# Weight casts, sums and the second spread at the end of the first attention take other places in the order

## The chip, the cores and the metric

The kernel runs on one core of one Trainium2 chip. The metric is the device time of one execution in microseconds (us), the median of several runs. The core has five engines that run side by side and meet at semaphores: TensorE (PE in the profile) multiplies, VectorE (DVE) and ScalarE (ACT) work on elements, GpSimd (POOL) and SyncE (SP) mostly issue transfers here. Each engine works off its own row of instructions strictly in the order in which they stand.

## What is computed

A model of two layers on 512 tokens of width 1024, in float32: a differential attention with a feed-forward block, then a sliding-window attention with sinks and a second feed-forward block. The change touches the end of the first attention. Cut to that:

```python
def one_block(args):                       # 128 queries of 8 heads, two maps c each
    s = jnp.einsum('bqhcd,bkhcd->bhcqk', qblk, k) * scale
    p = jax.nn.softmax(jnp.where(causal, s, NEG_INF), axis=-1)
    a = p[:, :, 0] - lam * p[:, :, 1]
    return jnp.einsum('bhqk,bkhe->bqhe', a, v)
...
o = rms_norm(o, subln) * (1.0 - lambda_init)
x = x + o.reshape(B, S, DA_V) @ w_o
x = x + swiglu(rms_norm(x, ffn_norm[l]), w_gate_up[l], w_down[l])
```

## The kernel before, in words

Every float32 product is made of three fast ones: each operand is split into a high part (`hi`, a cast on ScalarE) and a low part (`lo`, the rest, a subtraction on VectorE), and `mm3` (L295) multiplies high by high, high by low and low by high. Tokens are four blocks `t` of 128.

The first attention runs over four pairs of heads. For each pair a table of slots (`DA_STEPS`, for the last pair `DA_STEPS3`) gives the order of its steps on TensorE: T turns keys, C scores a block of queries, U transposes the differences of the two maps, W weighs the values, N sums the squares for the norm's root, B spreads the root over the rows. Between the steps other products are pulled in as filling. For the last pair the filling is the output projection of the first half (pairs 0 and 1, `o_da(0, ...)`, all four blocks) and of the second half (pairs 2 and 3, `o_da(1, ...)`) for blocks 0 and 1 once the outputs are there. Blocks 2 and 3 of the second half come behind the last step, mixed with the norms (`ffn.norm`) and turns (`ffn.turn`) of the feed-forward block, which then starts with `ffn.start`.

TensorE's row is as the code is written. VectorE's and ScalarE's rows are made by a scheduler: it goes by priorities (`tc.high_priority`) and by `tc.issue_after`, which puts an instruction behind another.

The names that the prediction speaks of, with lines:

- The **root**: `rsq` (L235 to L250), a chain of small VectorE steps on the sums `so` that ends in `ro`. `spread` (L1144) lets TensorE spread `ro` over the rows (`po`, L1148), and VectorE scales the output with it (`osb`, L1149).
- The **exponentials**: `soften` (L1077) gets the row maxima `mx` (taken by VectorE at L1071, scaled at L1080), ScalarE makes four exponentials of 128x512 for the last block of queries (L1084), VectorE the **difference** of the two maps (L1092). TensorE transposes it (L1108, banks `tr`), ScalarE and VectorE copy the result out as high and low parts (`aT`, L302 and L303). The next transposes into a bank wait for its copies. `weigh` (L1115) multiplies the values with `aT`.
- The **sums into x**: `o_block` (L457) multiplies one block into two banks `acc` (the halves `n` of the width), each with four pieces `j` of three products, and VectorE adds each bank to `xs` (L468).
- The **weight units**: `o_units` (L452) loads a half's part of `w_o` as four units of 128x2x512: pieces 0 and 1 for `n` = 0, the same for `n` = 1, pieces 2 and 3 for `n` = 0, then for `n` = 1. `load_w` (L281) issues each transfer into a raw buffer (L287), and `parts` makes two high parts (L269) and two low parts (L270) of it. The raw buffers form a ring of two, `tag="raw", bufs=RAWB` with `RAWB = 2` (L43): a transfer waits until the parts of the unit two before it are made.
- The **turned halves**: `transpose_in` (L310) turns a normed token block with TensorE (L314) and copies it out as `hTh` and `hTl` (L302, L303); `norm` (L520) squares on ScalarE (L526), takes a root, and multiplies on VectorE (L532). `start` (L594) is the first reader of the halves.

Of the kernel before, what the change touches and what calls it, by code (L numbers as in the profile page):

```python
# [40 lines left out]
HOT = 1220  # L41
# [71 lines left out]


# [23 lines left out]
def tile_yoco_hybrid(  # L138
# [96 lines left out]
    def rsq(dst, v, n):  # L235
        y = small([P, 32], "rsq_y", bufs=1)[:, 0:n] if n > 4 else small([P, 4], "rsq_s", bufs=2)[:, 0:n]
        w = small([P, 32], "rsq_w", bufs=1)[:, 0:n] if n > 4 else small([P, 4], "rsq_t", bufs=2)[:, 0:n]
        eng = nc.vector
        if n == 1:
            h = small([P, 1], "rsq_h")  # L240
            eng.tensor_scalar(h, v, -0.5, None, op0=ALU.mult)
        eng.tensor_scalar(w.bitcast(I32), v.bitcast(I32), 1, None, op0=ALU.logical_shift_right)
        eng.tensor_scalar(y.bitcast(I32), w.bitcast(I32), -1.0, float(0x5F3759DF), op0=ALU.mult, op1=ALU.add)
        for it in range(3):
            if n == 1:
                eng.tensor_scalar(w, y, y, h, op0=ALU.mult, op1=ALU.mult)
# [3 lines left out]
            eng.scalar_tensor_tensor(dst if it == 2 else y, w, 1.5, y, op0=ALU.add, op1=ALU.mult)  # L250

    class Split:

# [200 lines left out]
        return {(j, n): load_w([wv[:, k0 + j:k0 + j + 2, n * 512:(n + 1) * 512]], 2, 512)  # L454
                for j in (0, 2) for n in range(2)}

    def o_block(units, pieces, t, ready=None):  # L457
        while ready and not ready():
            yield None
        for n in range(2):  # L460
# [3 lines left out]
                mm3(pt, sh, sl, *units[j - j % 2, n].row(j % 2), j == 0, j == 3)  # L464
                yield 0.65
            xsl = xs[:, t, n * 512:(n + 1) * 512]
            with tc.high_priority(offset=HOT):
                nc.vector.tensor_tensor(xsl, xsl, pt, op=ALU.add)  # L468


    class Flow:
# [521 lines left out]
    class Pair:  # L993
# [83 lines left out]
        def soften(self, i):  # L1077
# [3 lines left out]
            for h in range(2):  # L1081
                for c in range(2):
                    g = 2 * h + c
                    nc.scalar.activation(sb[h][:, c, 0:n], sb[h][:, c, 0:n], AF.Exp, bias=mx[:, g:g + 1],  # L1084
                                         scale=self.scl[:, i, g:g + 1], accum_out=sm[:, g:g + 1])
            rs = small([P, 2], "rs2")
            nc.vector.reciprocal(rs, sm[:, 1::2])
            cl = small([P, 2], "cl")
            nc.vector.scalar_tensor_tensor(cl, rs, nlam, sm[:, 0::2], op0=ALU.mult, op1=ALU.mult)
            for h in range(2):  # L1090
                p0, p1 = sb[h][:, 0, 0:n], sb[h][:, 1, 0:n]
                nc.vector.scalar_tensor_tensor(p0, p1, cl[:, h:h + 1], p0, op0=ALU.mult, op1=ALU.add)  # L1092
            hf = i // 2
            if i % 2 == 0:
                self.eps[hf] = small([P, 4], "eps", bufs=3)
# [37 lines left out]
        def norm(self, hf):  # L1133
# [5 lines left out]
                nc.vector.scalar_tensor_tensor(so, pss[:, 0:8:2], 1.0 / P, self.eps[hf], op0=ALU.mult, op1=ALU.add)  # L1139
            self.ro = small([P, 4], "ro")  # L1140
            with tc.high_priority(offset=NPRI):
                rsq(self.ro, so, 4)

        def spread(self, hf):  # L1144
            pb = att("po")
# [15 lines left out]
    with tc.tile_pool(name="da", bufs=1, reuse_waits="tile") as ap:  # L1161
# [405 lines left out]
```

## Time and profile before

| what | before |
|---|---|
| median of 3 runs | 1122.76 us (1122.44 to 1123.15) |
| the profiled execution's own time | 1122.68 us |
| its span | 1120.6 us |
| busy in 225 to 275 us: PE, DVE, ACT | 47.52, 41.62, 26.17 us of 50 |
| last pair's last scores on TensorE | 229.85 us |
| first product of the second half's projection | 244.40 us |
| first product of the feed-forward block | 270.02 us |

In the order of time a row gives start, duration, engine, line, operation, output and inputs with their size, how many, and in brackets how long the engine had been idle before it and what ended the wait. In the table by stretches the columns are the stretch, its length, the busy time of PE, of its weight loads (PEld), DVE, ACT and POOL with the number of instructions, the granted clock of TensorE (1 is full), the busy share of the DMA engines and GB/s. L is a line of the kernel before.

### The profile page before, as it was taken

How to read it: one execution, taken by the hardware profiler on the slowest of the kernel's cores; microseconds unless marked ns; L12 is line 12 of the kernel's file. 1: busy time of each engine (PE TensorE's matmuls, PEld its weight loads, DVE VectorE, ACT ScalarE, POOL GpSimd, SP SyncE). 2: the span in 40 equal slices, each digit the busy share in tenths (PEclk: the TensorE clock that was granted, in tenths of full speed). 3: DMA queues.
4: the chain of work that ended last, by engine and by line, in shares of the span. 5: the costliest groups of instructions: out<-in, count | busy, mean ns of one | idle time of the engine just before them, and what ended most of it. 6: DMA issues, size and time to landing. Idle time of an engine off the chain costs nothing.

```text
span 1120.6 us, 20161 instructions
## 1 busy us (share of the span) xinstructions
PE 1101.9 (98%) x7206; PEld 979.5 (87%) x7206; DVE 1007.9 (90%) x2418; ACT 709.4 (63%) x1575; POOL 54.6 (5%) x76
## 2 busy tenths in 40 slices
PE   9999999999999999999999999999999999999998
PEld 7878888778989989989998778778989999998997
DVE  5979798979999999999998787988899999899997
ACT  5565756454556675675677499697555675566574
POOL 0100000000000010010003000000010000000000
PEclk9999999999999999999999999999999999999999
DMA  6312121224453444336124311120545247246213
GB/s 199 113 57 76 39 77 48 67 69 137 151 158 100 143 87 156 114 84 199 58 48 106 112 39 57 39 76 26 198 136 168 76 104 213 79 104 178 77 30 103
DMA packets 94085, 114.90 MB, mean 103 GB/s; under 512 B 5993, under 2 KB 70914, under 8 KB 93986
## 3 DMA queue, kind: packets, MB, share of 16 engines
q1 hardware_dynamic: 87216, 100.97, 28.0%
q0 software_dynamic: 6720, 12.65, 6.3%
q8 instruction: 56, 0.92, 0.3%
q14 instruction: 43, 0.35, 0.1%
q10 hardware_dynamic: 50, 0.01, 0.0%
HBM read 99.98 MB, written 2.10 MB: 91 GB/s over the span
## 4 chain that ended last, share of the span: by engine, by line
PE 81%; DVE 12%; ACT 6%; issue 1%; POOL 0%; DVEq 0%; ACTq 0%; POOLq 0%
PE acc L725 18%; PE tr L725 12%; PE tr L813 10%; PE acc L813 8%; PE acc L296 8%; PE acc L297 7%; PE acc L298 7%; PE po L725 2%; ACT s L1420 2%; PE tr L439 2%; DVE hss L389 1%; ACT s L1427 1%; DVE lo L270 1%; DVE u L405 1%; PE po L813 1%
## 5 line engine op out<-in xcount | busy, mean ns | idle before, releaser
L589 ACT CAST hi<-r 128x512 fp32r<-128x512 f32 x160 | 98.9, 620 | 78.9 <-PE acc L725 34.2
L296 PE MATMUL acc<-hi,hTh 128*128 128x512 f32 (+1 forms) x352 | 133.1, 378 | 2.2 <-DVE vl L1029 2.2
L297 PE MATMUL acc<-lo,hTh 128*128 128x512 f32 (+1 forms) x352 | 124.4, 354 | 0.4 <-DVE lo L270 0.4
L298 PE MATMUL acc<-hi,hTl 128*128 128x512 f32 (+1 forms) x352 | 124.4, 354 | 0.0
L589 ACT CAST hi<-g 128x512 fp32r<-128x512 f32 x154 | 94.9, 618 | 40.6 <-PE acc L297 19.2
L591 DVE TENSOR_TENSOR lo<-r,hi 128x512 fp32r<-128x512 f32 x160 | 104.8, 685 | 5.8 <-ACT hi L589 5.4
L589 ACT CAST hi<-raw 128x512 fp32r<-128x512 f32 x108 | 66.9, 620 | 61.5 <-PE tr L725 19.0
L796 ACT CAST ah<-lf 128x256 fp32r<-128x256 f32 x154 | 61.2, 404 | 47.2 <-PE tr L813 14.7
L725 PE MATMUL acc<-hTh,lo 128*128 128x256 f32 x288 | 81.5, 283 | 0.0
L725 PE MATMUL acc<-hTl,hi 128*128 128x256 f32 x288 | 81.5, 283 | 0.0
L725 PE MATMUL acc<-hTh,hi 128*128 128x256 f32 x288 | 81.4, 283 | 0.0
L725 PE MATMUL acc<-tl,hi 128*128 128x256 f32 x288 | 81.1, 282 | 0.0
L725 PE MATMUL acc<-th,hi 128*128 128x256 f32 x288 | 81.1, 281 | 0.0
L725 PE MATMUL acc<-th,lo 128*128 128x256 f32 x288 | 81.0, 281 | 0.0
L296 PEld LDWEIGHTS acc<-hi,hTh 128*128 128x128 f32 x352 | 66.9, 190 | 12.9 <-issue 2.6
L269 ACT CAST hi<-raw 128x512 fp32r<-128x512 f32 x96 | 57.4, 619 | 30.8 <-PE acc L298 17.6
L591 DVE TENSOR_TENSOR lo<-g,hi 128x512 fp32r<-128x512 f32 x110 | 75.2, 684 | 1.5 <-ACT hi L589 1.4
L298 PEld LDWEIGHTS acc<-hi,hTl 128*128 128x128 f32 x352 | 66.8, 190 | 9.5
L588 POOL DMA_DIRECT2D lo<-g x44 | 38.5, 975 | 715.1 <-ACT lo L587 308.4
L297 PEld LDWEIGHTS acc<-lo,hTh 128*128 128x128 f32 x352 | 67.1, 191 | 6.7 <-DVE lo L270 0.7
L591 DVE TENSOR_TENSOR lo<-raw,hi 128x512 fp32r<-128x512 f32 x108 | 72.7, 685 | 0.0
L270 DVE TENSOR_TENSOR lo<-raw,hi 128x512 fp32r<-128x512 f32 x96 | 64.4, 684 | 6.7 <-ACT hi L269 6.3
(278 smaller groups left out, 3635.0 us busy)
## 6 DMA issues: line engine op xcount, KB each, us to landing
r<-in_w_gate_up_dram SPq DMA_DIRECT2D x80, 512.0 KB, 4.9
g<-in_w_down_dram SPq DMA_DIRECT2D x88, 256.0 KB, 5.3
lo<-g POOLq DMA_DIRECT2D x44, 256.0 KB, 3.8
raw<-in_da_w_qkv_dram SPq DMA_DIRECT2D x30, 256.0 KB, 3.1
raw<-in_da_w_qkv_dram SPq DMA_DIRECT2D x8, 512.0 KB, 4.0
raw<-in_da_w_o_dram SPq DMA_DIRECT2D x8, 512.0 KB, 3.7
raw<-in_w_gate_up_dram SPq DMA_DIRECT2D x8, 512.0 KB, 3.7
raw<-in_sw_w_o_dram SPq DMA_DIRECT2D x8, 512.0 KB, 3.7
```

The costliest lines, as they stand in the source:

```text
L269: nc.scalar.copy(hi, part)
L270: nc.vector.tensor_tensor(lo, part, hi.bitcast(F32), op=ALU.subtract)
L296: nc.tensor.matmul(dst, sh, mh, start=start, stop=False)
L297: nc.tensor.matmul(dst, sh, ml, start=False, stop=False)
L298: nc.tensor.matmul(dst, sl, mh, start=False, stop=stop)
L439: nc.tensor.matmul(banks[c][:, cols], q[a][rows], k[b][rows], start=a + b == 0, stop=a == 1)
L588: nc.gpsimd.dma_start(out=lo.bitcast(F32), in_=src, accum_op=ALU.add)
L589: nc.scalar.copy(hi, src)
L591: nc.vector.tensor_tensor(lo, src, hi.bitcast(F32), op=ALU.subtract)
L725: nc.tensor.matmul(dst, l[:, k, :], r[:, k, :], start=fresh and k == 0 and i == 0, stop=k == 3 and i == 2, skip_group_check=not fresh)
L796: nc.scalar.copy(ah, src)
L813: nc.tensor.matmul(bank, l[:, tk], r, start=fresh and i == 0 and n == 0, stop=i == len(qs) - 1 and n == 2, skip_group_check=not fresh)
```

## The change

Five edits:

1. `rsq` returns its last instruction, and the pair keeps it (`rooted`), the last exponential (`raised`) and the last difference (`mixed`).
2. The parts of all four weight units of the second half are put behind the last pair's first root and its last exponential.
3. Two sums into `xs` are put behind other VectorE work: that of block 2, `n` = 1 behind the root, and that of block 3, `n` = 0 behind the difference (both of the first half's projection).
4. The second spread B of the last pair moves from slot 56.9 to 58.6.
5. Block 2 of the second half takes a new routine, `o_block2`: pair 2's pieces for both halves of the width first, then pair 3's.

```diff
         (48.6, N, 1),
-        (56.9, B, 1),
+        (58.6, B, 1),
...
-            eng.scalar_tensor_tensor(dst if it == 2 else y, w, 1.5, y, op0=ALU.add, op1=ALU.mult)
+            last = eng.scalar_tensor_tensor(dst if it == 2 else y, w, 1.5, y, op0=ALU.add, op1=ALU.mult)
+        return last
...
-    def o_block(units, pieces, t, ready=None):
+    def o_block(units, pieces, t, ready=None, after=lambda t, n: None):
...
-            with tc.high_priority(offset=HOT):
+            with tc.high_priority(offset=HOT), ExitStack() as hold:
+                if after(t, n):
+                    hold.enter_context(tc.issue_after(after(t, n)))
                 nc.vector.tensor_tensor(xsl, xsl, pt, op=ALU.add)
+
+    def o_block2(units, pieces, t, order):
+
+        banks = {}
+        for n, half in order:
+            if n not in banks:
+                banks[n] = acc()
+            for j in (2 * half, 2 * half + 1):
+                mm3(banks[n], *pieces(j, t), *units[2 * half, n].row(j % 2), j == 0, j == 3)
+                yield n, j
+            if half:
+                xsl = xs[:, t, n * 512:(n + 1) * 512]
+                with tc.high_priority(offset=HOT):
+                    nc.vector.tensor_tensor(xsl, xsl, banks[n], op=ALU.add)
...
+        def after_da(t, n):
+            return {(2, 1): lambda: pairs[3].rooted.ins, (3, 0): lambda: pairs[3].mixed.ins}.get((t, n), lambda: None)()
+
         def o_da(half, ts, ready=None):
             if half not in da_units:
-                da_units[half] = o_units(da_w_o[0], 4 * half)
+                with ExitStack() as hold:
+                    if half:
+                        hold.enter_context(tc.issue_after(pairs[3].rooted.ins))
+                        hold.enter_context(tc.issue_after(pairs[3].raised.ins))
+                    da_units[half] = o_units(da_w_o[0], 4 * half)
             for t in ts:
-                yield from o_block(da_units[half], pieces_da(half), t, ready)
+                yield from o_block(da_units[half], pieces_da(half), t, ready, (after_da, lambda t, n: None)[half])
...
-        run(o_da(1, (2,)))
+        run(o_block2(da_units[1], pieces_da(1), 2, ((0, 0), (1, 0), (0, 1), (1, 1))))
```

The rows of the engines show where this puts the instructions. Line numbers of the changed kernel are a few higher.

VectorE's row before, at the last pair's first root (`rsq`, `ro`): `acc_624` is block 2's second sum, `mx` the scaled maxima of the last scores, `lo_656` and `lo_658` the low parts of the first unit (`raw_654`).

```order
L468 TENSOR_TENSOR xs_76<-xs_76,acc_624_3009 128x512
L250 SCALAR_TENSOR_TENSOR rsq_s_628_3027<-rsq_t_629_3028,rsq_s_628_3027 128x4
L1080 SCALAR_TENSOR_TENSOR mx_615_2974<-mx_615_2974,hscl_492_2419 128x4
L270 TENSOR_TENSOR lo_656_3178<-raw_654_3175,hi_655_3177 128x512
L248 TENSOR_TENSOR rsq_t_629_3028<-rsq_s_628_3027 128x4
L270 TENSOR_TENSOR lo_658_3182<-raw_654_3175,hi_657_3181 128x512
L249 SCALAR_TENSOR_TENSOR rsq_t_629_3028<-rsq_t_629_3028,so_626_3024 128x4
L250 SCALAR_TENSOR_TENSOR ro_627_3026<-rsq_t_629_3028,rsq_s_628_3027 128x4
```

The same place with the change:

```order
L250 SCALAR_TENSOR_TENSOR rsq_s_628_3027<-rsq_t_629_3028,rsq_s_628_3027 128x4
L1097 SCALAR_TENSOR_TENSOR mx_615_2974<-mx_615_2974,hscl_492_2419 128x4
L248 TENSOR_TENSOR rsq_t_629_3028<-rsq_s_628_3027 128x4
L249 SCALAR_TENSOR_TENSOR rsq_t_629_3028<-rsq_t_629_3028,so_626_3024 128x4
L250 SCALAR_TENSOR_TENSOR ro_627_3026<-rsq_t_629_3028,rsq_s_628_3027 128x4
L471 TENSOR_TENSOR xs_76<-xs_76,acc_624_3009 128x512
```

One sum and two low parts left the stretch between the maxima and the end of the root. On ScalarE the two casts of the same unit left the place ahead of the four exponentials in the same way.

VectorE's row with the change, right behind the difference, to the low parts of the first weight unit. `tr_639`, `tr_647`, `tr_649` and `tr_650` are the transposes' banks, `acc_634` and `acc_648` block 3's two banks, `ol_642` the low part of an output, `raw_654` the first unit.

```order
L471 TENSOR_TENSOR xs_76<-xs_76,acc_634_3066 128x512
L304 TENSOR_TENSOR aT_638_3079<-tr_639_3080,aT_636_3077 128x128
L1171 TENSOR_TENSOR ol_642_3095<-osb_622_3004,oh_641_3094 128x512
L304 TENSOR_TENSOR aT_645_3103<-tr_647_3105,aT_643_3101 128x2x128
L304 TENSOR_TENSOR aT_645_3103<-tr_649_3118,aT_643_3101 128x2x128
L304 TENSOR_TENSOR aT_646_3104<-tr_647_3105,aT_644_3102 128x128
L304 TENSOR_TENSOR aT_637_3078<-tr_650_3130,aT_635_3076 128x2x128
L471 TENSOR_TENSOR xs_76<-xs_76,acc_648_3114 128x512
L304 TENSOR_TENSOR aT_646_3104<-tr_649_3118,aT_644_3102 128x2x128
L304 TENSOR_TENSOR aT_638_3079<-tr_650_3130,aT_636_3077 128x2x128
L271 TENSOR_TENSOR lo_656_3178<-raw_654_3175,hi_655_3177 128x512
L271 TENSOR_TENSOR lo_658_3182<-raw_654_3175,hi_657_3181 128x512
```

Before, the end of this place read (`raw_659` and `raw_664` are the second and the third unit):

```order
L303 TENSOR_TENSOR aT_646_3104<-tr_649_3118,aT_644_3102 128x2x128
L468 TENSOR_TENSOR xs_76<-xs_76,acc_648_3114 128x512
L303 TENSOR_TENSOR aT_637_3078<-tr_650_3130,aT_635_3076 128x2x128
L270 TENSOR_TENSOR lo_663_3192<-raw_659_3185,hi_662_3191 128x512
L303 TENSOR_TENSOR aT_638_3079<-tr_650_3130,aT_636_3077 128x2x128
L270 TENSOR_TENSOR lo_666_3198<-raw_664_3195,hi_665_3197 128x512
```

The low parts of the first two units moved behind all the copies, and block 3's two sums moved ahead of copies that stood before them.

VectorE's row before, where the second token block's turned halves are copied out (`hTl` from `tr_712` and `tr_713`), followed by the same place with the change. `xn_705` is the third block's norm, `acc_711` the last block's second sum.

```order
L303 TENSOR_TENSOR hTl_687_3303<-tr_712_3421,hTh_686_3302 128x4x128
L246 TENSOR_SCALAR rsq_t_708_3390<-rsq_s_707_3389,rsq_h_709_3391 128x1
L468 TENSOR_TENSOR xs_76<-xs_76,acc_711_3417 128x512
L250 SCALAR_TENSOR_TENSOR rsq_s_707_3389<-rsq_t_708_3390,rsq_s_707_3389 128x1
L303 TENSOR_TENSOR hTl_687_3303<-tr_713_3428,hTh_686_3302 128x4x128
```

```order
L304 TENSOR_TENSOR hTl_687_3303<-tr_712_3421,hTh_686_3302 128x4x128
L250 SCALAR_TENSOR_TENSOR frr_706_3388<-rsq_t_708_3390,rsq_s_707_3389 128x1
L471 TENSOR_TENSOR xs_76<-xs_76,acc_711_3417 128x512
L549 SCALAR_TENSOR_TENSOR xn_705_3385<-xs_76,frr_706_3388,gb_539_2671 128x512
L549 SCALAR_TENSOR_TENSOR xn_705_3385<-xs_76,frr_706_3388,gb_540_2673 128x512
L544 TENSOR_SCALAR fss_714_3445<-fss_714_3445 128x1
L304 TENSOR_TENSOR hTl_687_3303<-tr_713_3428,hTh_686_3302 128x4x128
```

The third block's root is further on when the first of the two copies comes, and its two products of the norm moved ahead of the second.

More of the change, by code (lines that the diff above doesn't have):

```diff
@@ L1083, in soften @@
                     g = 2 * h + c
-                    nc.scalar.activation(sb[h][:, c, 0:n], sb[h][:, c, 0:n], AF.Exp, bias=mx[:, g:g + 1],
-                                         scale=self.scl[:, i, g:g + 1], accum_out=sm[:, g:g + 1])
+                    self.raised = nc.scalar.activation(sb[h][:, c, 0:n], sb[h][:, c, 0:n], AF.Exp, bias=mx[:, g:g + 1],
+                                                       scale=self.scl[:, i, g:g + 1], accum_out=sm[:, g:g + 1])
             rs = small([P, 2], "rs2")
@@ L1091, in soften @@
                 p0, p1 = sb[h][:, 0, 0:n], sb[h][:, 1, 0:n]
-                nc.vector.scalar_tensor_tensor(p0, p1, cl[:, h:h + 1], p0, op0=ALU.mult, op1=ALU.add)
+                self.mixed = nc.vector.scalar_tensor_tensor(p0, p1, cl[:, h:h + 1], p0, op0=ALU.mult, op1=ALU.add)
             hf = i // 2
@@ L1141, in norm @@
             with tc.high_priority(offset=NPRI):
-                rsq(self.ro, so, 4)
+                self.rooted = rsq(self.ro, so, 4)
         def spread(self, hf):
```

## The prediction

> **What bounds the kernel now.** I read the page first, then busy time by stretches, then the order of time on each engine around 225 to 275 us, where the first attention's last pair ends.
>
> ```profile
> span 1120.6 us, 20161 instructions
> PE 1101.9 (98%) x7206; PEld 979.5 (87%) x7206; DVE 1007.9 (90%) x2418; ACT 709.4 (63%) x1575; POOL 54.6 (5%) x76
> 275.00:320.00 45.00, 45.00 (x281) 40.70 (x280) 43.11 (x68) 22.96 (x41) 1.83 (x2) 1.00 0.56 175
> 500.00:600.00 100.00, 100.00 (x683) 93.08 (x682) 95.51 (x179) 65.43 (x136) 9.05 (x11) 1.00 0.37 99
> ```
>
> TensorE (PE) is the bound: 1101.9 of 1120.6 us. From 275 us on it has no idle time for hundreds of us (the last two rows bound that stretch). So whatever TensorE loses or gains before 275 us goes one for one into the end. The profiled execution took 1122.68 us: its span and 2.08 us around it. The median of the runs is 1122.76. I add shifts of TensorE to 1122.68.
>
> In the stage that the change touches TensorE waits three times:
>
> ```profile
> 233.60 0.49 PE L1108 MATMUL tr<-ident,s 128*128 128x128 f32 x3
> 235.05 0.62 PE L1148 MATMUL po<-ident,ro 128*128 128x128 f32 x4 [0.96 <-DVE ro L250]
> 238.56 0.66 PE L1108 MATMUL tr<-ident,s 128*128 128x128 f32 x4 [1.15 <-DVE s L1092]
> 239.74 0.60 PE L1108 MATMUL tr<-ident,s 128*128 128x128 f32 x4
> 242.40 0.28 PE L297 MATMUL po<-aT,vh 128*128 128x256 f32 x1
> 245.83 0.39 PE L296 MATMUL acc<-hi,oh 128*128 128x512 f32 x1
> 246.06 0.39 PE L297 MATMUL acc<-lo,oh 128*128 128x512 f32 x1
> 252.75 0.62 PE L1148 MATMUL po<-ident,ro 128*128 128x128 f32 x4 [0.37 <-DVE ro L250]
> 270.19 0.39 PE L297 MATMUL acc<-hTl,hi 128*128 128x256 f32 x1
> ```
>
> 0.96 + 1.15 + 0.37 = 2.48 us is all that the change can win there. The last row lasted 0.39 where a product of its size takes 0.28 (the row of 242.40): TensorE just met its operand, so VectorE (DVE) has no slack at 270 us.
>
> **Root and exponentials.**
>
> ```profile
> 231.93 0.68 DVE L1071 CUSTOM_DVE_ANT_0 s<-tr,maskD 128x512 f32<-128x512 f32 x1
> 232.54 0.68 DVE L468 TENSOR_TENSOR xs<-xs,acc 128x512 f32<-128x512 f32 x1
> 233.21 0.15 DVE L1080 SCALAR_TENSOR_TENSOR mx<-mx,hscl 128x4 f32<-128x4 f32 x1
> 233.28 0.68 DVE L270 TENSOR_TENSOR lo<-raw,hi 128x512 fp32r<-128x512 f32 x1
> 234.75 0.16 DVE L250 SCALAR_TENSOR_TENSOR ro<-rsq_t,rsq_s 128x4 f32<-128x4 f32 x1
> 237.75 1.41 DVE L1092 SCALAR_TENSOR_TENSOR s<-s,cl 128x512 f32<-128x512 f32 x2
> 239.08 0.29 DVE L303 TENSOR_TENSOR aT<-tr,aT 128x128 fp32r<-128x128 f32 x1
> 232.44 1.30 ACT L269 CAST hi<-raw 128x512 fp32r<-128x512 f32 x2 [4.05 <-PE acc L298]
> 233.65 0.81 ACT L1084 ACTIVATE s<-s,mx,hscl 128x512 f32<-128x512 f32 x1
> ```
>
> One sum (232.54) and two low parts (233.28 and its fellow) leave the root's way, 0.60 us of its row each: the root is done near 233.2 instead of 234.91 (a little later than 234.91 - 1.8, since its small steps now wait on each other). TensorE comes to the spread by itself at 235.05 - 0.96 = 234.09, so the whole 0.96 goes. On ScalarE (ACT) two casts leave the way of the exponentials. The scaled maxima (233.21) come 0.60 earlier without the sum, ready at 232.76, so the exponentials start near 232.9 instead of 233.65, where the casts had held them: 0.75 earlier, and with them the difference (237.75) and the transposes behind it. The wait at 238.56 is therefore not removed: TensorE is now early there and waits 1.36 instead of 1.15. Behind it TensorE stands **0.75 ahead**.
>
> **What is late next on VectorE.** The sum of the fourth block now stands right behind the difference, ahead of the copy of 239.08. That copy frees the bank of the transposes at 239.74. Its end, 239.37, becomes 239.37 - 0.75 + 0.60 = 239.22, and the transposes follow 0.1 later at 239.32: **0.4 ahead**. Next in VectorE's row the sum of the block that TensorE is just finishing comes before the last copies of the transposed differences:
>
> ```profile
> 241.14 0.69 DVE L303 TENSOR_TENSOR aT<-tr,aT 128x128 fp32r<-128x128 f32 x2
> 241.77 0.69 DVE L468 TENSOR_TENSOR xs<-xs,acc 128x512 f32<-128x512 f32 x1
> 242.37 0.42 DVE L303 TENSOR_TENSOR aT<-tr,aT 128x256 fp32r<-128x256 f32 x1
> 242.71 0.68 DVE L270 TENSOR_TENSOR lo<-raw,hi 128x512 fp32r<-128x512 f32 x1
> ```
>
> Before, the second copy at 241.14 ran ahead of the sum. Now the sum starts at 241.77 - 0.4 = 241.37 (it waits for TensorE's block), the copy at 241.97, ends at 242.39 (0.42), and the product that reads it starts at 242.5, where it stood at 242.40: **0.1 behind**. What the root and the exponentials won is spent.
>
> **The main cost: the third weight unit.** The four weight units of the second half share a ring of two raw buffers. The third unit's transfer can only start when both low parts of the first are done. Those two ran at 233.28 and close behind it and now stand behind all the copies: another copy at 242.31, low parts at 242.64 and 243.24, the second ending at 243.24 + 0.68 = 243.92. What comes then is seen before on the fourth unit:
>
> ```profile
> 243.45 0.37 SPq L287 DMA_DIRECT2D raw<-in_da_w_o_dram  x1
> DMA to landing us min/median/max: 3.4/3.6/4.8
> 247.07 1.14 ACT L269 CAST hi<-raw 128x512 fp32r<-128x512 f32 x2 [1.16 <-DMA raw<-in_da_w_o_dram]
> 247.72 0.69 DVE L270 TENSOR_TENSOR lo<-raw,hi 128x512 fp32r<-128x512 f32 x1 [2.80 <-ACT hi L269]
> ```
>
> A low part ended at 243.39 (242.71 + 0.68), the transfer was issued 0.06 later, the cast started 3.62 after that. The same steps from 243.92: issue 243.98, cast 247.60, done 248.22 (0.62), TensorE 248.32. It reads this part at 245.83 in the rows above, now 245.93: a wait of 2.4 us, **2.5 behind**. The low part of the same unit starts at 248.3, ends at 248.98, and its product runs at 249.06 instead of 246.06: **3.0 behind**. The fourth unit's transfer, issued near 245.2, lands near 248.9 and its parts are done by 250.1 and 252, ahead of TensorE's 252.5: no cost. Bounds of the transfer: 3.4 to 4.8 us, so -0.2 to +1.2; I take 3.62, the same weight from the same tensor.
>
> A rule beside it: the Trainium skill, "DMA: Bandwidth & Descriptors", section "Anatomy of one DMA", gives 2.0 us and bytes over 436e3 for a transfer issued by GpSimd; for this unit's 512 KB that is an estimate of 3.2 us and would take 0.4 off the wait. The row of 3.62 decides.
>
> **The moved spread.** The second spread goes behind three more products (0.68 us), beyond the 0.37 that it waited. Its root is then ready about 0.6 ahead of TensorE. That is 0.37 won: **2.63 behind**.
>
> **The clock.** The trace has one wait of this length:
>
> ```profile
> 46.70 0.79 PE L296 MATMUL acc<-hi,hTh 128*128 128x512 f32 x1 [2.16 <-DVE vl L1029]
> 46.00:48.00 2.00, 1.30 (x3) 1.11 (x4) 2.00 (x7) 0.82 (x3) 0.00 (x0) 0.63 0.11 38
> 48.00:50.00 2.00, 2.00 (x8) 1.51 (x8) 2.00 (x4) 0.40 (x1) 0.00 (x0) 0.52 0.00 0
> 225.00:235.00 10.00, 9.09 (x53) 7.37 (x52) 8.06 (x30) 5.87 (x15) 0.29 (x1) 1.00 0.00 0
> 235.00:245.00 10.00, 8.80 (x57) 7.63 (x58) 9.17 (x21) 7.04 (x20) 0.00 (x0) 1.00 0.19 56
> ```
>
> After 2.16 us without work the granted clock, the third number from the end, fell to 0.63 and 0.52 in two stretches of 2 us. That costs (0.37 + 0.48) x 2 = 1.70 us. The waits of 0.96 and 1.15 lie in the last two stretches and did not do this (clock 1.00). The new wait, 2.4 and then 0.5 more, is longer than the one that did. Bounds: 0 (no fall) and 1.70; part of the slow stretch lies over the second wait, so I take **1.45: 4.1 behind**.
>
> A rule against that term: the Trainium skill, "TensorE: Matmul & The Clock Gate", section "Part 1: The HAM clock gate", says that the clock halves after at least one idle window of about 3.4 us. By that, 2.4 us would not do it; the row of 2.16 us shows that less than a whole window did. It stays as a rival below.
>
> **The turned halves.** VectorE makes the low halves of the second turned token block just in time before (270.19).
>
> ```profile
> 262.82 1.41 DVE L532 SCALAR_TENSOR_TENSOR xn<-xs,frr,gb 128x512 f32<-128x512 f32 x2
> 269.45 0.69 DVE L303 TENSOR_TENSOR hTl<-tr,hTh 128x512 fp32r<-128x512 f32 x1
> 270.23 0.68 DVE L468 TENSOR_TENSOR xs<-xs,acc 128x512 f32<-128x512 f32 x1
> 270.90 0.69 DVE L303 TENSOR_TENSOR hTl<-tr,hTh 128x512 fp32r<-128x512 f32 x1
> ```
>
> In the new row three steps of a root (0.45 us of spacing) come ahead of the first of them, and some steps that were hidden between wide ones wait on each other: some 0.9 in all, of which 0.35 is covered because VectorE's chain into this place is less late than TensorE. That is 0.55. Ahead of the second stand a sum (0.60) and two products of the norm (0.67 each, half of 1.41 less the overlap): it follows the first by 2.68 instead of 1.45, 1.23 more, of which I take 1.15. Bounds for both: 0, if VectorE has gained slack earlier, and 2.1. I take **1.7**.
>
> **The sum:** -0.75 + 0.35 + 0.5 (copies) + 2.9 (unit) - 0.37 + 1.45 + 1.7 = 5.78. 1122.68 + 5.8 = **1128.4 us**. The new block routine gives the same 24 products and the same two sums, and only puts six of them earlier that need no new operand; TensorE did not wait in that block before, so it is worth nothing here.
>
> **Rivals.** (1) The clock holds: all else as above, 1122.68 + 2.63 + 1.7 = 1127.0. For it: a single row shows the fall. (2) The late halves are covered: 1122.68 + 2.63 + 1.45 = 1126.8. For it: a long wait of TensorE lets VectorE empty its row. Against: the same row stands behind it, and had no slack. (3) A slow transfer, 4.8 us, the slowest of the four: 1.2 more, 1129.6. (4) Not slower: the third unit lands in time. It would have to be issued by 245.93 - 0.1 - 0.62 - 3.62 = 241.6, so the low parts of the first unit would have to end 2.3 us before my 243.92. Then neither the wait nor the clock counts: 0.1 - 0.37 + 1.7 = 1.4, or 1124.1, within 0.2%. For it: ScalarE makes the high parts early, near 237. Against: VectorE is in order, and a sum that needs TensorE's block at 241.37 stands ahead of the low parts. (5) The change does what it says and all three waits go: 1122.68 - 2.48 = 1120.2. Against: the difference wins only 0.75 of its 1.15, and 0.85 of that is lost behind the two sums.
>
> **Chances.** Forecast 0.50; (1) 0.20; (2) 0.12; (3) 0.07; (4) 0.08; (5) 0.03. About 0.2%, 2.2 us, is what a measurement of this kernel can tell from no change: slower is above 1125.0, faster below 1120.5. Forecast and (1) to (3) are slower, 0.89; (4) is the same, 0.08; (5) faster, 0.03. The range leaves out (4) and (5), 0.11. Its lower end takes (1) and (2) together, 1125.3; its upper end is (3): 1125.2 to 1129.7.
>
> **What would show it.** In the new profile: the spread near 234.1 without a wait; exponentials from 232.9; the transposes behind the difference near 237.8, with a longer wait than 1.15; the cast of the third unit near 247.6, released by its transfer; TensorE idle over 2 us near 246 to 248; a granted clock of about one half behind it; the second spread without a wait; waits of about 0.5 and 1.2 at the low halves near 274 and 277. I am wrong if the third unit's transfer is issued before 242, or if TensorE does not wait for it.

## The result, and the profile after

The changed kernel took 1130.28 us (median of 7 runs, 1128.42 to 1130.82), the kernel before 1123.15 us in the same session (7 runs, 1122.29 to 1127.8): a ratio of 1.0053, with a 95% interval of 1.0036 to 1.0069. The change makes the kernel slower. The forecast was 1128.4 us; the direction and the mechanism held, but the time came out 1.9 us later and 0.6 us beyond the upper end of the range.

The page of the changed kernel, first lines. The profiled execution took 1130.28 us:

```profile
span 1128.2 us, 20159 instructions
PE 1105.6 (98%) x7206; PEld 981.9 (87%) x7206; DVE 1009.3 (89%) x2418; ACT 709.9 (63%) x1575; POOL 54.8 (5%) x76
```

TensorE is still the bound, so its shifts are again the whole account. The order of time on TensorE in the changed kernel (start, duration, what it is, in brackets the idle time before it and what ended it):

```profile
228.20 0.95 PE L1153 MATMUL po<-ones,osq 128*128 128x2 f32 x8
...
233.16 0.60 PE L1165 MATMUL po<-ident,ro 128*128 128x128 f32 x4
...
236.88 0.66 PE L1125 MATMUL tr<-ident,s 128*128 128x128 f32 x4 [1.39 <-DVE s L1109]
238.43 0.63 PE L1125 MATMUL tr<-ident,s 128*128 128x128 f32 x4 [0.20 <-DVE aT L304]
241.55 0.38 PE L298 MATMUL po<-aT,vh 128*128 128x256 f32 x1 [0.29 <-DVE aT L304]
248.66 0.49 PE L297 MATMUL acc<-hi,oh 128*128 128x512 f32 x1 [3.48 <-ACT hi L270]
249.39 0.50 PE L298 MATMUL acc<-lo,oh 128*128 128x512 f32 x1 [0.23 <-DVE lo L271]
259.54 0.60 PE L1165 MATMUL po<-ident,ro 128*128 128x128 f32 x4
260.67 0.40 PE L297 MATMUL acc<-hi,oh 128*128 128x512 f32 x1
276.80 0.39 PE L298 MATMUL acc<-hTl,hi 128*128 128x256 f32 x1 [0.45 <-DVE hTl L304]
279.45 0.39 PE L298 MATMUL acc<-hTl,hi 128*128 128x256 f32 x1 [0.97 <-DVE hTl L304]
```

Three rows of the kernel before, from the same view, serve as marks: the first product of the stage, one product behind the slow stretch, and the reader of the second low half.

```profile
228.98 0.95 PE L1136 MATMUL po<-ones,osq 128*128 128x2 f32 x8
...
254.61 0.39 PE L296 MATMUL acc<-hi,oh 128*128 128x512 f32 x1
...
271.74 0.29 PE L297 MATMUL acc<-hTl,hi 128*128 128x256 f32 x1
```

The changed kernel enters the stage 0.78 us early (228.20 against 228.98). That is no doing of the change: in this execution the clock held at the wait near 46 us, where it fell in the profiled execution of the kernel before. (In the run alone, whose rows are the changed kernel's, it fell there too, and the stage began 0.29 late.) So 0.78 is added to each difference below. Counted so, TensorE stands 0.90 ahead at the transposes of 236.88, 0.53 ahead at those of 238.43, 0.07 ahead at the product of 241.55, 3.61 behind at the third unit's product, 4.11 behind at its low part, 6.84 behind at the product of 260.67, 7.39 behind at the first low half and 8.49 at the second. 8.49 - 0.78 = 7.71 is the difference of the two spans, 1128.2 - 1120.6 = 7.6, to 0.1.

The late unit, in the order of time on SyncE, VectorE and ScalarE of the changed kernel:

```profile
241.75 2.49 DVE L271 TENSOR_TENSOR lo<-raw,hi 128x512 fp32r<-128x512 f32 x4
243.09 1.57 SPq L288 DMA_DIRECT2D raw<-in_da_w_o_dram  x2
247.99 2.37 ACT L270 CAST hi<-raw 128x512 fp32r<-128x512 f32 x4 [2.91 <-DMA raw<-in_da_w_o_dram]
```

The first two of the four low parts end near 243.0, the transfer that needs their buffer goes out at 243.09, and its cast starts at 247.99, 4.90 us later. TensorE waits 3.48 for it.

The clock, by stretches of the changed kernel (busy time of each engine; the third number from the end is the granted clock):

```profile
45.37:48.78 3.41, 1.99 (x11) 1.68 (x12) 3.41 (x11) 1.92 (x4) 0.00 (x0) 1.00 0.26 84
...
243.34:246.75 3.41, 1.84 (x10) 1.23 (x9) 0.89 (x2) 1.22 (x2) 0.00 (x0) 1.00 0.62 182
246.75:250.17 3.42, 1.28 (x4) 0.85 (x5) 1.53 (x3) 2.08 (x4) 0.00 (x0) 1.00 0.35 130
250.17:253.58 3.41, 3.41 (x13) 3.04 (x13) 1.87 (x5) 0.19 (x1) 0.00 (x0) 0.50 0.49 154
253.58:257.00 3.42, 3.42 (x9) 2.64 (x8) 1.04 (x7) 0.00 (x0) 0.00 (x0) 0.50 0.49 153
257.00:260.41 3.41, 3.41 (x18) 2.83 (x17) 1.97 (x11) 1.15 (x2) 0.00 (x0) 1.00 0.00 0
```

It is one half for 6.83 us behind the wait, twice as long as in the kernel before at 46 us, and back at 1.00 from 257.00 on.

### The profile page after: what moved, and what is told of

Its sections match the earlier page's. It is cut to its first block, busy times and chain, and to the rows that moved or that the text cites. A ratio compares the mean times of both kernels' runs of the same rounds, so it can differ in the third digit from the quotient of the medians.

```text
span 1128.2 us, 20159 instructions
## 1 busy us (share of the span) xinstructions
PE 1105.6 (98%) x7206; PEld 981.9 (87%) x7206; DVE 1009.3 (89%) x2418; ACT 709.9 (63%) x1575; POOL 54.8 (5%) x76
## 4 chain that ended last, share of the span: by engine, by line
PE 75%; DVE 15%; ACT 6%; DMA 2%; issue 1%; POOL 0%; SPq 0%; DVEq 0%; ACTq 0%; POOLq 0%
PE acc L742 16%; PE tr L742 10%; PE tr L830 9%; PE acc L830 8%; PE acc L297 7%; PE acc L298 7%; PE acc L299 7%; PE po L742 2%; ACT s L1444 2%; PE tr L440 2%; DVE lo L271 1%; DVE hss L390 1%; ACT s L1451 1%; DVE u L406 1%; DMA r<-in_w_gate_up_dram 1%
```

## The experiments

**Theory:** the low parts of the first unit stand late in VectorE's row, so the third unit's transfer waits for its buffer in the ring of two; TensorE waits for it, and that wait brings the clock down. **Rivals:** VectorE's full row holds TensorE in any case; the clock falls without the wait; only one of the two moves is to blame. Ratios are against the kernel before, run in between on the same chip.

**own_buffer.** The third unit gets a raw buffer of its own, and its transfer goes out right behind the second unit's. The units behind it take the ring's two places one step earlier; the rest of the change is as it was.

```diff
-raw = wp.tile([P, a, b], F32, name=nm("raw"), tag="raw", bufs=RAWB)
+raw = wp.tile([P, a, b], F32, name=nm("raw"), tag=tag, bufs=RAWB if tag == "raw" else 1)
...
+tag="raw3" if (j, n) == (2, 0) else "raw", past=units[0, 1].dma.ins if (j, n) == (2, 0) else None
```

> The changed kernel, but the third weight unit of the second half has a raw buffer of its own, so its transfer need not wait for the low parts of the first unit (it is issued right behind the second unit's). Theory (the late transfer in the ring of two holds TensorE, and that wait lets the clock fall): the transfer is issued before 240, its cast runs long before 246, the product of the third unit no longer waits for the cast (3.48 before) nor its low part (0.23), and the granted clock stays 1.00 from 245 to 260. The sum: 1130.3 - 3.6 (unit) - 0.5 (low part) - 3.1 (clock) + 0.9 (VectorE's row behind it now has less time, so the waits at the low halves grow from 0.45 and 0.97 to about 1.5 and 1.2) = 1124.0, within 1122.8 to 1125.5. Rival A (VectorE's full row, not the buffer, holds the third unit): the wait stays over 2 us and the time over 1128.5. Rival B (the clock falls at this place without the wait): the wait goes but the clock is 0.5 for some us, 1126 to 1127.5.

1123.97 us against 1123.67, ratio 1.0003 (0.9993 to 1.0013). TensorE's waits in own_buffer between 225 and 285 us, all of them:

```profile
237.74 0.66 PE L1133 MATMUL tr<-ident,s 128*128 128x128 f32 x4 [1.39 <-DVE s L1117]
239.29 0.63 PE L1133 MATMUL tr<-ident,s 128*128 128x128 f32 x4 [0.20 <-DVE aT L307]
242.41 0.39 PE L301 MATMUL po<-aT,vh 128*128 128x256 f32 x1 [0.29 <-DVE aT L307]
270.48 0.39 PE L301 MATMUL acc<-hTl,hi 128*128 128x256 f32 x1 [0.70 <-DVE hTl L307]
273.14 0.39 PE L301 MATMUL acc<-hTl,hi 128*128 128x256 f32 x1 [0.96 <-DVE hTl L307]
```

The waits of 3.48 and 0.23 are gone, the clock is 1.00 through the stage, and the loss with them. This shows the buffer as the cause of the wait, and VectorE's row as no bound of its own at the third unit. The waits at the low halves, 0.70 and 0.96, stayed below the 1.5 and 1.2 expected. What is left is TensorE 0.29 behind at the first low half (270.48 against 270.19) and the wait of 0.96 at the second: 1.2 us, as the spans say (1121.7 against 1120.6), and inside the interval. So the rest of the change brings nothing that can be measured.

**keep_busy.** The data come late as before, but TensorE has work in the wait whose results nobody reads: 26 transposes of the identity.

```diff
 sh, sl = pieces(j, t)
+if keep and (t, n, j) == (0, 0, 2):
+    busy(keep)
 mm3(pt, sh, sl, *units[j - j % 2, n].row(j % 2), j == 0, j == 3)
```

> The changed kernel with 26 transposes of the identity put on TensorE ahead of the first product of the third unit, into a bank that nobody reads: about 0.11 us each (four of them take 0.60 with their latency of some 0.28), 2.9 us of the 3.48 that TensorE waits there. Theory: the wait for the data is the same and the third unit's product starts as late as before (about 3.6 us behind the kernel before), but the granted clock stays at 1.00, and the 3.1 us of the slow stretch go: 1130.3 - 3.1 = 1127.2, within 1126.3 to 1128.5. Rival A (the clock has nothing to do with this wait): the clock falls all the same, 1130.3. Rival B (VectorE's row would have held TensorE anyway, so the slow clock was covered): the clock stays 1.00, but the waits at the low halves grow by 2 to 3 us, 1129 to 1130.3.

1127.73 us, ratio 1.0036 (1.0023 to 1.0048). TensorE in keep_busy at the third unit, in order of time:

```profile
245.76 3.00 PE L219 MATMUL po<-ident 128*128 128x128 f32 x26
248.94 0.50 PE L297 MATMUL acc<-hi,oh 128*128 128x512 f32 x1 [0.17 <-ACT hi L270]
249.66 0.50 PE L298 MATMUL acc<-lo,oh 128*128 128x512 f32 x1 [0.23 <-DVE lo L271]
```

The data are nearly as late as before (the third unit's product is 3.11 behind, against 3.61), and the granted clock was 1.00 all the way to 285 us. Over the whole run it was 0.998 in all five runs, against 0.994 to 0.998 in the seven of the changed kernel. So the fall of the clock comes from TensorE's idleness. The ratio fell from 1.0053 to 1.0036, which is about 2 us; by the medians the loss fell from 7.1 to 4.1 us, and in the profiled execution the clock cost 3.1. The two intervals overlap, so what the clock costs on average is known only roughly.

**plain_block.** The new block routine undone, the rest kept.

```diff
-run(o_block2(da_units[1], pieces_da(1), 2, ((0, 0), (1, 0), (0, 1), (1, 1))))
+run(o_da(1, (2,)))
```

> The changed kernel with the third token block's projection of the second half in its old order (the new routine undone, the other edits kept). Theory (the routine is worth nothing: TensorE did not wait in that block, and has come far behind VectorE's operands there): 1130.3, within 1129.5 to 1131, the wait of 3.48 and the slow clock unchanged. Rival A (the routine covers a late operand): slower by 0.5 to 1.5, a wait at the block's first products of the second pair half. Rival B (its two banks and the later first sum cost): faster by 0.5 to 1.5, with the waits at the low halves (0.45, 0.97) smaller.

1131.10 us, ratio 1.0067 (1.0054 to 1.0079): the interval overlaps that of the whole change, and the time lies 0.1 above the range expected. The wait at the third unit is there (2.65), and the clock was one half for 10.2 us. The routine is worth nothing that can be measured, neither way.

**sums_alone, hold_alone, one_sum.** Which of the moves makes the unit late? The first has the two held sums without the holding of the weight parts (the slot and the routine stay), the second the holding alone, the third the whole change but for one of the two sums.

```diff
# sums_alone: the changed kernel without
-hold.enter_context(tc.issue_after(pairs[3].rooted.ins))
-hold.enter_context(tc.issue_after(pairs[3].raised.ins))
# hold_alone: the changed kernel without sums, block routine and slot
-return {(2, 1): lambda: pairs[3].rooted.ins, (3, 0): lambda: pairs[3].mixed.ins}.get((t, n), lambda: None)()
+return {}.get((t, n), lambda: None)()
# one_sum: the changed kernel with
+return {(2, 1): lambda: pairs[3].rooted.ins}.get((t, n), lambda: None)()
```

> The changed kernel without the holding of the weight parts: the casts and low parts of the second half are no longer put behind the root and the exponentials; the two held sums and the new block routine stay. Theory (VectorE's row is so full here that either edit alone puts the first unit's second low part behind the late copies): VectorE's row now has the first low part ahead of the differences but the second still behind the last copies, so the third unit's transfer is issued only some 0.6 us earlier than the 243.1 to 244.2 seen, TensorE still waits over 2 us for its cast, and the clock falls for one to three windows of 3.4 us. 1129.5, within 1127.5 to 1131. Rival (only the holding of the parts makes the transfer late; without it the ring is free in time): issue before 241.6, no wait for the cast, 1124 to 1125.5.

> The kernel before with one edit only: the weight parts of the second half are put behind the root and the exponentials (no held sums, the old block routine, the slot as before). Theory: the holding alone puts both low parts of the first unit behind copies, the transfer comes within 0.7 us of where the whole change has it, TensorE waits over 2 us, the clock falls for one to three windows: 1129.4, within 1127.5 to 1131. Rival (the sums ahead of the copies are what makes the low parts late): wait for the third unit's cast below 1 us, no fall of the clock, 1124 to 1125.5.

> The changed kernel with one sum held instead of two: the sum behind the difference goes back to its old place, the one behind the root stays. In VectorE's row both low parts of the first unit then stand ahead of the sum that waits for TensorE's block, about 1.6 us earlier than in the changed kernel. Theory (the wait shrinks with the issue of that transfer, and a wait below the 2.16 us of the start does not bring the clock down): transfer issued near 241.8, wait for the cast 1.0 to 1.9, granted clock 1.00 from 245 to 260, the low halves still late by about 1.6: 1126.9, within 1125.5 to 1128.3. Rival A (the clock falls after a shorter wait too): 1128.5 to 1130. Rival B (the place of this sum does not matter): wait over 3 us, 1130.

sums_alone 1129.60 us, ratio 1.0049 (1.0032 to 1.0065); hold_alone 1131.10, ratio 1.0056 (1.0039 to 1.0072); one_sum 1125.06, ratio 1.0014 (1.0005 to 1.0022). The third unit's product in sums_alone, from the order of time on TensorE:

```profile
248.80 0.50 PE L297 MATMUL acc<-hi,oh 128*128 128x512 f32 x1 [2.40 <-ACT hi L270]
```

The same product in hold_alone:

```profile
247.88 0.50 PE L297 MATMUL acc<-hi,oh 128*128 128x512 f32 x1 [1.93 <-ACT hi L270]
```

And one_sum, the transfer on SyncE, its cast on ScalarE, and the only wait of TensorE at this unit:

```profile
241.76 2.89 SPq L288 DMA_DIRECT2D raw<-in_da_w_o_dram  x2
245.55 1.14 ACT L270 CAST hi<-raw 128x512 fp32r<-128x512 f32 x2 [4.04 <-DMA raw<-in_da_w_o_dram]
246.95 0.50 PE L298 MATMUL acc<-lo,oh 128*128 128x512 f32 x1 [0.22 <-DVE lo L271]
```

Either move alone brings nearly the whole loss, and the two together not more: it is one late transfer, issued at 243.70 in sums_alone and at 243.40 in hold_alone, and each of the moves is enough to make it late. With the second sum back in its old place the transfer goes out at 241.76 instead of 243.09 (2.2 us earlier, counted from the entry into the stage), the long wait is gone, the clock holds, and 0.14% is left. A wait for the cast of 1.0 to 1.9 us and a time of 1125.5 us or more had been expected here; there was no wait for the cast, since this transfer took 3.79 us.

**alone, apart, apart_again, changed_again.** Why 4.90 us instead of 3.62? The fourth unit's transfer follows 1.2 us behind. In alone it was to be issued behind the third unit's cast, but that only orders the issue on SyncE's queue and adds no wait, and the queue had this order before: every engine's row in alone is that of the changed kernel, so it is the changed kernel once more. In apart it goes through ScalarE's queue, behind the cast.

```diff
+past = units[2, 0].cast.ins if apart and (j, n) == (2, 1) else None
...
-nc.sync.dma_start(out=raw[:, :, i * w:(i + 1) * w], in_=src)
+with ExitStack() as hold:
+    if past is not None:
+        hold.enter_context(tc.issue_after(past))
+    (nc.sync if past is None else nc.scalar).dma_start(out=raw[:, :, i * w:(i + 1) * w], in_=src)
```

> The changed kernel, with the fourth unit's transfer issued only behind the third unit's first cast, so that the third's has the DMA engines to itself. Theory (two transfers 1.2 us apart share the engines: 4.9 us from issue to cast where one alone took 3.62): the third unit's cast comes 1.2 us earlier after the issue, the wait of 3.48 falls to about 2.3. The clock then falls for one window of 3.4 us or for two: 1130.3 - 1.2 = 1129.1 with two, 1127.4 with one. The fourth unit lands near 250.5, and may cost up to 0.5 of that at its own product. Rival (this transfer is as slow by itself at this time): still 4.9 us, wait 3.4, 1130.3.

> The changed kernel with the fourth unit's transfer issued from ScalarE's queue behind the third unit's two casts, so that the third's transfer runs alone. So far the time from issue to cast was 4.07 to 4.90 us where the next transfer was issued 1.2 us behind (five runs) and 3.62 to 3.84 where it came 1.5 us behind or later, or not at all (four). Theory (they share the DMA engines): 3.6 to 3.9 from issue to cast, the wait for the cast 0.4 to 1.2 us shorter than the 3.17 and 3.48 seen. Rival (it is slow for another reason at this time, such as the transfer's own tensor or the queue): 4.1 to 4.9 still. The total tells little here, since the fourth unit now comes late.

> The kernel of the run apart once more (the fourth unit's transfer behind the third unit's casts), for a second look at the third unit's transfer, which took 4.24 us from issue to cast in the first, between the two groups. Theory (the transfers share the engines): 3.6 to 4.2. Rival (this transfer is slow at this place without the other): 4.2 to 4.9. For the clock: by the runs so far it runs in windows of 3.413 us and falls at the end of one in which TensorE was idle for more than about half (1.83 us and more fell, 1.70 and less did not). If that holds, it tells for this run from the phase of its windows whether the wait of some 2.8 us brings the clock down: it does if over 1.8 us of it lie in one window.

> The changed kernel once more, as the other side of apart_again. Theory of sharing: 4.1 to 4.9 us from issue to cast of the third unit, the next transfer 1.2 us behind; rival: as in apart_again. Clock: the wait at the third unit is 2.6 to 3.5 us, so the clock falls unless it is cut in two halves below 1.8 us by the edge of a window.

alone took 1131.99 us, ratio 1.0072 (1.0058 to 1.0085), with a cast 4.58 us behind the issue; changed_again 1130.06, with 4.27. With the transfer by itself the cast came 4.24 us (apart, 1127.44 us) and 4.73 us (apart_again, 1130.79 us) behind the issue; apart, apart_again and changed_again are single runs, and in the first two TensorE waited another 1.12 and 1.14 us for the fourth unit, which now came late. The theory of sharing falls for the third unit: alone or not, this transfer took 4.07 to 4.90 us in eight runs, and 3.59 to 3.84 in five others (the third unit in one_sum and hold_alone, the fourth in the kernel before, own_buffer and own_hold). It does hold for the fourth: that landed 4.55 to 4.99 us behind its issue where it followed 1.2 us behind the third (six runs), and 3.62 and 3.65 where it came behind the casts.

What goes with it stands in the list of DMA queues, taken from a transfer's issue to its cast; its columns are packets, megabytes, and the time that the packets took as a share of the 16 engines' span. The changed kernel (243.09 to 247.99) has a queue of instructions in it:

```profile
q8 instruction: 1, 0.02, 2.1%
```

The same of plain_block (244.14 to 248.21):

```profile
q8 instruction: 1, 0.02, 1.4%
```

And of one_sum (241.76 to 245.55), where the queue of the transfers is the only one:

```profile
q1 hardware_dynamic: 291, 0.56, 49.0%
```

In each of the eight slow cases one packet of instructions starts within 2 us behind the issue; in the five others there is none by then. It holds one engine of 16 for 2.1% x 16 x 4.90 = 1.6 us in the slowest case and 1.4% x 16 x 4.07 = 0.9 us in the quickest of the eight, and if the transfer has a share on that engine, it is only done when that share is. Beyond these thirteen the traces agree less sharply. Take every transfer of the two output projections' weights, in all fourteen traces, that had no other issued in the 4.5 us before it. Twelve had such a packet beside them for 0.3 us or more between 1.0 and 2.5 us behind the issue, and landed after 3.71 to 4.88 us, in the median 4.43. The 107 that had none there took 3.48 to 4.36, in the median 3.74. So the packet goes with a slow transfer, but not always and not only. No experiment moved the packet itself; that it is the cause was only argued.

**own_hold.** The holding and the buffer of own_buffer, on the kernel before.

> The kernel before with two edits: the weight parts held behind the root and the exponentials, and a raw buffer of its own for the third unit (no held sums, old block routine, old slot). Theory (the low halves at 270 are late where VectorE's row has steps of the next root and a norm ahead of them, which the held sums and the later slot bring; the holding alone does not): no wait at the third unit, clock 1.00 from 245 to 260, the second low half follows the first by about 1.45 as in the kernel before (270.90 after 269.45) and TensorE waits under 0.5 at the first and not at the second. The holding itself wins 0.2 at the transposes behind the difference: the same time as the kernel before, 0 to 0.4 us less, within -0.8 to +0.8 of it. Rival (the holding brings the late halves too): waits of about 0.7 and 1.0 there, 1.2 to 1.6 us more than the kernel before.

1123.13 us against 1123.76, ratio 0.9994 (0.9985 to 1.0002). VectorE's low halves of the second turned block in own_hold, in order of time:

```profile
271.40 0.69 DVE L307 TENSOR_TENSOR hTl<-tr,hTh 128x512 fp32r<-128x512 f32 x1
272.85 0.69 DVE L307 TENSOR_TENSOR hTl<-tr,hTh 128x512 fp32r<-128x512 f32 x1
```

The same place in own_buffer:

```profile
269.75 0.68 DVE L307 TENSOR_TENSOR hTl<-tr,hTh 128x512 fp32r<-128x512 f32 x1
...
271.01 1.41 DVE L557 SCALAR_TENSOR_TENSOR xn<-xs,frr,gb 128x512 f32<-128x512 f32 x2
272.41 0.68 DVE L307 TENSOR_TENSOR hTl<-tr,hTh 128x512 fp32r<-128x512 f32 x1
```

They start 1.45 us apart as in the kernel before, against 2.66 with the norm's two products between them; own_hold has no wait at either. So the order of VectorE's row makes these waits. Which edit brings that order is less plain than expected: hold_alone, without any held sum, has the wait of 0.96 as well. As far as the measurement tells, own_hold is as fast as the kernel before; it beats the changed kernel, and nothing beat the kernel before.

**best_of.** An attempt at more: the extra buffer, one held sum, no holding, and four low parts of the feed-forward's first weights on GpSimd to empty VectorE's row.

```diff
-nc.vector.tensor_tensor(lo, part, hi.bitcast(F32), op=ALU.subtract)
+(low or nc.vector).tensor_tensor(lo, part, hi.bitcast(F32), op=ALU.subtract)
```

> A version made from what the runs so far show: third weight units have a raw buffer of their own (as in own_buffer, and the third unit of the feed-forward part uses the same buffer), the weight parts are not held, one sum is held behind the root, the old block routine and slot, and the second low halves of the feed-forward's first four units are made on GpSimd instead of VectorE (a 128x256 product took 1.02 us there, so about 2 us each). Theory (what is left is VectorE's row, which is full from 263 to 276): the root and the exponentials win 0.8 us at the transposes, no wait at the third unit, no clock fall, and the waits at the low halves (0.70 and 0.96 in own_buffer) go because two low parts leave VectorE's row ahead of them: 1.3 us below the kernel before, 1122.1 where that has 1123.4, within 1121.0 to 1124.0. Rival (GpSimd's work slows VectorE's beside it, or its parts come late): a new wait between 270 and 285, 1124 or more.

1125.05 us against 1124.33, ratio 1.0006 (0.9997 to 1.0015): nothing won. GpSimd in best_of, in order of time:

```profile
266.10 4.73 POOL L271 TENSOR_TENSOR lo<-raw,hi 128x512 fp32r<-128x512 f32 x3 [32.78 <-ACT hi L270]
```

VectorE beside and behind it:

```profile
268.11 1.59 DVE L271 TENSOR_TENSOR lo<-raw,hi 128x512 fp32r<-128x512 f32 x1
269.63 1.21 DVE L250 SCALAR_TENSOR_TENSOR rsq_s<-rsq_t,rsq_s 128x1 f32<-128x1 f32 x1
270.77 0.68 DVE L307 TENSOR_TENSOR hTl<-tr,hTh 128x512 fp32r<-128x512 f32 x1
```

And TensorE at the low half:

```profile
271.50 0.38 PE L301 MATMUL acc<-hTl,hi 128*128 128x256 f32 x1 [1.83 <-DVE hTl L307]
```

VectorE's low part beside GpSimd's took 1.59 instead of 0.68 and a root step on one column 1.21 instead of 0.15, some 2 us in all. That is what VectorE's row was relieved of by the three low parts that GpSimd made up to there (about 0.6 us each). TensorE waited 1.83 for the low half, and the clock fell for 3.4 us behind it.

## Why the prediction came out as it did

By its own steps, the forecast first and then what the changed kernel showed, with the entry's 0.78 added:

| step | forecast, us behind | measured |
|---|---|---|
| transposes behind the difference | -0.75 | -0.90 |
| next transposes (copy behind the first sum) | -0.4 | -0.53 |
| product on the last copies | 0.1 | -0.07 |
| third unit | 2.5 | 3.61 |
| its low part | 3.0 | 4.11 |
| clock, less the second spread's wait | 4.1 | 6.84 |
| first low half | 4.65 | 7.39 |
| second low half | 5.8 | 8.49 |

**What held:** the root's wait goes (233.16, no wait); the difference wins less than a microsecond; the two sums take it back; the first unit's low parts end late, at 243.0 + 0.78 against the forecast's 243.92, and the transfer goes out at 243.09 + 0.78 against 243.98; the low halves cost 0.55 and 1.10 where 0.55 and 1.15 stood. That the first of these came out to the hundredth is luck: the wait at it was 0.45 here, 0.27 in plain_block and 0.70 in own_buffer, while that at the second was 0.96 or 0.97 in each. The second spread lost its wait (259.54). own_buffer shows the late unit as the heart of it; what the low halves cost beyond the win at the transposes is too little to measure there. The routine's zero is borne out by plain_block within the measurement.

**What failed: two terms of the sum were too small, the third unit's transfer and the clock.** The transfer was put at 3.62 us, with 4.8 as its upper bound; it took 4.90, and in the eight runs in which it stood behind both held sums it never took under 4.07. That is 1.3 of transfer and 1.1 of TensorE. The row of 3.62 was a single reading, of the same tensor a little later, without an instruction packet near its start; what makes the third unit's transfer longer stays open. The clock was put at 1.45, with 1.70 as its bound: 6.84 - 4.11 + 0.37 = 3.10 was measured. The bound took the only slow stretch seen, one of 3.4 us, for the longest that can follow. Runs here had none, one, two and three stretches of that length behind one wait. The range's upper end took the slow transfer alone, without a longer fall of the clock. Together 1.1 + 1.65 = 2.75 are missing. 0.78 of it does not show in the total, since the profiled execution began without the fall at 46 us that the one before had; what is left of it, 1.9 to 2.0, is the miss.

**The rivals.** (1), that the clock holds (1127.0), was not what the profiled runs of the changed kernel showed, but apart had it, with a wait of 2.83 us, and so it is a chance of each run rather than a property of the kernel. (2), that the late halves are covered, was not seen: they cost 0.55 and 1.10. (3), the slow transfer (1129.6), is what came, and the longer fall of the clock came on top of it. (4), the third unit in time (1124.1), is what one_sum and own_buffer gave, 1125.06 and 1123.97: the condition named there, an issue by about 241.6, was the right one. (5), that all three waits go, fails at the transposes, where the wait grew to 1.39. The prediction held the holding of the low parts for what is late; hold_alone and sums_alone show that the sums alone do it too.

## What to carry to other kernels

A step that is moved later takes with it the buffers that it frees: ask of each ring which transfer waits for the moved step, and when that must land, before counting what the move wins. When two moves each delay the same transfer, undoing one of them recovers little, and a buffer, or an order that lets the one releasing step through, recovers nearly all. In this kernel a wait of TensorE of about 2 us or more should be priced with a clock loss of 0 to 5 us, by chance, beside its own length: up to three stretches of 3.41 us at half clock were seen behind one wait.

## What the runs showed of the hardware

**The clock goes by windows of 3.413 us that run free of the program.** Every stretch of one clock between the first and the last is a multiple of it, in the thirteen profiled runs that have one, and the edges lie elsewhere in each run. The changed kernel's rows by these windows stand in the result; here the kernel before at its wait of 2.16:

```profile
43.11:46.52 3.41, 1.42 (x12) 1.22 (x11) 3.41 (x16) 2.59 (x6) 0.00 (x0) 1.00 0.80 248
46.52:49.93 3.41, 3.23 (x9) 2.55 (x10) 3.41 (x8) 1.14 (x2) 0.00 (x0) 0.50 0.01 5
```

And apart at its wait of 2.83:

```profile
243.26:246.67 3.41, 1.88 (x11) 1.27 (x9) 0.94 (x2) 1.22 (x2) 0.00 (x0) 1.00 0.54 158
246.67:250.08 3.41, 1.88 (x8) 1.33 (x8) 1.29 (x2) 1.14 (x2) 0.00 (x0) 1.00 0.43 139
```

In the kernel before, 3.41 - 1.42 = 1.99 us of a window were idle, and the clock fell at its end. In apart the window's edge cut the wait in two (1.53 idle in each window), and it held. Up to the last products of the program, windows with 1.83 us idle or more (best_of's is the shortest) all ended in a fall; of those with 1.74 (hold_alone's) or less, only one did: changed_again's, with 1.63, against the rule that was written ahead of it. In the window of the last products two with 1.9 us idle (best_of, apart_again) did not end in a fall. So about half a window decides, with a margin that these runs don't settle, and the same wait can cost or not by its place against the edge. The times of one kernel go with this: hold_alone took 1125.52 us with a granted clock of 1.000 over the run, and 1132.44 with 0.993. The Trainium skill, "TensorE: Matmul & The Clock Gate", section "Part 1: The HAM clock gate", names the free-running window of 3413 ns, which these rows bear out. Its rule that the clock halves after at least one idle window they don't: about half a window was enough. Why one, two or three slow windows follow stays open.

**GpSimd holds VectorE up, and VectorE GpSimd.** In best_of the stretched instructions of VectorE are those with two inputs in SBUF. The sum of 266.33, which reads a bank in PSUM, kept its time beside GpSimd's first product (266.10 to 267.39); the root step behind it took 0.48 instead of 0.15, until that product ended. GpSimd's second product then took 1.82 where its first took 1.29.

```profile
266.33 0.68 DVE L479 TENSOR_TENSOR xs<-xs,acc 128x512 f32<-128x512 f32 x1
266.92 0.48 DVE L250 SCALAR_TENSOR_TENSOR rsq_s<-rsq_t,rsq_s 128x1 f32<-128x1 f32 x1
267.34 1.82 POOL L271 TENSOR_TENSOR lo<-raw,hi 128x512 fp32r<-128x512 f32 x1
```

The Trainium skill, "SBUF — State Buffer", section "SBUF: two separate sides", says that such an instruction and one of GpSimd that reads SBUF take a shared port for their whole length, and these rows agree.
